# Sums of FFN weight blocks: from VectorE instructions to accumulating DMAs issued by GpSimd

## The chip, the cores and the metric

The kernel runs on one core of a Trainium2 chip. The metric is the device time of one execution in microseconds. A core has TensorE (PE, matmuls; PEld is its weight load), VectorE (DVE), ScalarE (ACT), GpSimd (POOL) and SyncE (SP), which here issues all DMAs; 16 DMA engines carry them. Each engine works through its own queue in order, and waits at the head of it for the semaphores of others.

## The reference, cut to what matters

A two-layer encoder step (a Mamba-2 SSD layer, then an HGRN2 layer), each mixer followed by a SwiGLU FFN, for 1024 prompt tokens and 32 sample tokens, D_MODEL 1024, FFN_HIDDEN 2816, all in float32. The change is in the FFN:

```python
def swiglu(h, w_gate, w_up, w_down):
    return (jax.nn.silu(h @ w_gate) * (h @ w_up)) @ w_down
...
            x = x + out.astype(x.dtype)
            x = x + swiglu(rmsnorm(x, ffn_norm_w[layer]), ffn_w_gate[layer], ffn_w_up[layer], ffn_w_down[layer])
```

## The kernel before, in words

The 1056 tokens go in two halves of 512 and 544 columns; a half is split in two again, n = 256 or 272. Every float32 operand is split into a high and a low part (`wh`/`wl`, `xh`/`xl`), and a product is three matmuls: high by high, high by low, low by high.

The FFN's hidden columns come in 11 slabs of 256. In each half the first one or two slabs go the plain way (`ffn_head`). The others are computed as units, one for the gate and one for the up product: `ffn_unit` multiplies a weight block of 1024 x 256 by a half in Strassen's manner (Winograd's form). The weight slab is cut into four blocks a11, a12, a21, a22 of 512 x 128 (rows 0 to 511 or 512 to 1023, columns 0 to 127 or 128 to 255), the activations into four likewise, and seven products take the place of eight. Each of the seven is a `part`: 4 row blocks by 3 matmuls, 12 matmuls (lines 1003 to 1005). The activation side of the sums is made once for each half by `x_combos` (tiles `th`, `tl`); the weight side for each unit by `unit_weights`. There are 18 units in a first half and 20 in a second one, 76 in both layers, with 2128 x 3 matmuls.

`unit_raw` (line 959) loads the slab by two DMAs of 512 KB (rows of 1 KB) into two `raw` tiles, or into the one Y tile, in turn: gate units in `raw` (three slots), upper units in Y (one). `unit_weights` (line 973) then makes, with four VectorE instructions over 128 x 512, the sums s1 = a21 + a22, s3 = a11 - a21, s2 = s1 - a11 and s4 = a12 - s2, in place where it can, and hands out in the order a11, s1, a12, s2, s4, s3, a22 the split pairs: `hl` is one copy by ScalarE (`wh`, 128 x 512) and one subtraction by VectorE, into one of six `ws` slots. As all helpers call one function for each operation, line 101 of the profile stands for any VectorE `tensor_tensor`, line 98 for any ScalarE activation, line 104 for `scalar_tensor_tensor` and line 110 for any DMA.

`in_turn` interleaves the generators of two neighbouring units: parts 4 and 5 of one, part 1 of the next, part 6, parts 2 and 3, part 7. After each two slabs (four units, 28 parts) the down product of a pair of slabs, `ffn_outs`, comes in; it runs behind part 7 of the first gate unit of the pair that follows, with part 3 of the upper unit beside it already done. It needs four down weights of 512 KB (`wload`, a `raw` slot and two `ws` slots each) and has 96 matmuls of 512 columns in the first half, 192 of 272 in the second (lines 316 to 318).

The order on each engine is made by a planner from the order of the program, priorities and its own estimate of durations; a tile's slot is given on when its last reader is done. SP's queue holds all DMAs in that planned order. POOL issues none; its few instructions belong to the start and to the SSD layer.

Of the kernel before, what the change touches and what calls it, by code (L numbers as in the profile page):

```python
# [8 lines left out]
F32 = mybir.dt.float32  # L9
F32R = mybir.dt.float32r  # L10
U32 = mybir.dt.uint32
AF = mybir.ActivationFunctionType
# [4 lines left out]
P = 128  # L17
# [24 lines left out]
TW = 552  # L42
# [6 lines left out]
def trunk_kernel(ctx, tc, x_prompt, x_sample, state_ssd, cache_conv, state_hgrn,  # L49
# [5 lines left out]
    V, A, G, PE = nc.vector, nc.scalar, nc.gpsimd, nc.tensor  # L55
# [3 lines left out]
    wp = ctx.enter_context(tc.tile_pool(name="wp", bufs=1))  # L59
# [6 lines left out]
    def nm(s):  # L66
        uid[0] += 1
        return f"{s}_{uid[0]}"

    def T(tag, s, dt=F32):  # L70
        return tp.tile([P, WIDTH[tag]], dt, tag=tag, bufs=BUFS[tag], name=nm(s))
# [25 lines left out]
    def act(out, in_, f, **kw):  # L97
        A.activation(out=out, in_=in_, func=f, **kw)  # L98

    def tt(out, a, b, op, eng=None):  # L100
        (eng or V).tensor_tensor(out=out, in0=a, in1=b, op=op)  # L101

    def stt(out, a, s, b, op0, op1):
        V.scalar_tensor_tensor(out=out, in0=a, scalar=s, in1=b, op0=op0, op1=op1)  # L104
# [4 lines left out]
    def dma(out, in_):  # L109
        nc.sync.dma_start(out=out, in_=in_)  # L110
# [14 lines left out]
    MUL, ADD, SUB = ALU.mult, ALU.add, ALU.subtract  # L125
# [5 lines left out]
    def place(w):  # L131
        used[0] += -(-w // 16) * 16
        return fixed[:, used[0] - -(-w // 16) * 16:][:, :w]
# [23 lines left out]
    for i in range(2):  # L157
        t = place(P)
# [125 lines left out]
    def split(xf, w, pair):  # L284
        xh, xl = pair
        act(xh[:, :w], xf, AF.Copy)
        tt(xl[:, :w], xf, xh[:, :w].bitcast(F32), SUB)
        return pair
# [102 lines left out]
    st = [place(TW) for _ in range(NG)]  # L391
# [540 lines left out]
    def x_combos(h, xn, tx, kept=None):  # L932


        L, n = LEN[h], LEN[h] // 2

        def piece(k):
            xf = []
            for m in (k, k + 4):
                if kept:  # L940
                    xf.append(kept[m])
                    continue
                f = T("n", "xf")
                tt(f[:, :L], xn[m][0].bitcast(F32)[:, :L], xn[m][1].bitcast(F32)[:, :L], ADD)
                xf.append(f)
            b11, b12, b21, b22 = [f[:, q * n:(q + 1) * n] for f in xf for q in range(2)]
            t, u = T("w", "xt"), T("w", "xt")
            tt(t[:, :n], b12, b11, SUB)
            tt(t[:, n:L], b22, t[:, :n], SUB)
            tt(u[:, :n], b22, b12, SUB)  # L950
            tt(u[:, n:L], b21, t[:, n:L], SUB)
            for q, f in enumerate((t, u)):
                tags = [XN2[4 * k + 2 * q], XN2[4 * k + 2 * q + 1]]
                tx[2 * k + q] = split(f[:, :L], L, (T(tags[0], "th", F32R), T(tags[1], "tl", F32R)))
        return [lambda k=k: piece(k) for k in range(4)]

    NU = [0]

    def unit_raw(src):

        if NU[0] % 2:
            t = sp.tile([P, 4 * TW], F32, tag="Y", bufs=1, name=nm("raw2"))
            halves = [t[:, q * 1024:(q + 1) * 1024] for q in range(2)]
        else:
            halves = [wp.tile([P, 2 * TW], F32, tag="raw", bufs=3, name=nm("raw"))[:, :1024] for _ in range(2)]
        out = []
        for q in range(2):
            r3 = halves[q].rearrange("p (k c) -> p k c", k=4)
            dma(r3, src[q * 512:(q + 1) * 512, :].rearrange("(k p) c -> p k c", p=P))
            out.append([r3[:, :, i * P:(i + 1) * P] for i in range(2)])  # L970
        return out

    def unit_weights(src):

        (a11, a21), (a12, a22) = unit_raw(src)

        def hl(x):
            w = wp.tile([P, 2 * TW], F32R, tag="ws", bufs=6, name=nm("wh"))[:, :1024]
            v = w.rearrange("p (q k c) -> p q k c", q=2, k=4)
            act(v[:, 0], x, AF.Copy)  # L980
            tt(v[:, 1], x, v[:, 0].bitcast(F32), SUB)
            return v[:, 0], v[:, 1]

        NU[0] += 1
        s1 = st[NU[0] % 2][:, :512].rearrange("p (k c) -> p k c", k=4)
        yield hl(a11)
        tt(s1, a21, a22, ADD)
        yield hl(s1)
        yield hl(a12)
        tt(a21, a11, a21, SUB)  # L990
        tt(a11, s1, a11, SUB)
        yield hl(a11)
        tt(s1, a12, a11, SUB)
        yield hl(s1)
        yield hl(a21)
        yield hl(a22)

    def part(ps, n, w, xs, more):

# [7 lines left out]
    def ffn_unit(h, src, xn, tx, tag, after):  # L1007


        n = LEN[h] // 2  # L1010
        w = unit_weights(src)
        lo, hi = slice(0, n), slice(n, 2 * n)
        t12, t34 = tx[0::2], tx[1::2]
        px = psum_mm((0, 1))
        s12, s35 = T("n", "s12"), T("n", "s35")

        def of(tiles, q):
            return [(a[:, q * n:(q + 1) * n], b[:, q * n:(q + 1) * n]) for a, b in tiles]

        part(px, n, next(w), of(xn[:4], 0), False)  # L1020
        act(s12[:, lo], px[:, :n], AF.Copy)
        yield
        py, pz = psum_sc(), psum_sc()
        part(py, n, next(w), of(t12, 0), False)
        act(s35[:, hi], py[:, :n], AF.Copy)
        part(pz, n, next(w), of(xn[4:], 0), False)
        yield
        dst = [T(tag, "f" + tag) for _ in range(2)]
        tt(dst[0][:, lo], pz[:, :n], s12[:, lo], ADD)
        part(px, n, next(w), of(t12, 1), True)  # L1030
        act(s12[:, hi], px[:, :n], AF.Copy)
        part(py, n, next(w), of(xn[4:], 1), True)
        tt(dst[0][:, hi], py[:, :n], s12[:, hi], ADD)
        yield
        part(px, n, next(w), of(t34, 0), True)
        act(s35[:, lo], px[:, :n], AF.Copy)
        tt(dst[1][:, hi], s35[:, lo], s35[:, hi], ADD)
        yield
        part(px, n, next(w), of(t34, 1), True)
        act(dst[1][:, lo], px[:, :n], AF.Copy)  # L1040
        after(dst)
# [19 lines left out]
    def ffn_gate(layer, h, s, xn, tx, g):  # L1061
        L = LEN[h]

        def after(dst):
            g.extend(dst)
            for x in g:
                act(x[:, :L], x[:, :L], AF.Silu)
        return ffn_unit(h, ffn_w_gate[layer][:, s * 256:(s + 1) * 256], xn, tx, "w", after)

    def ffn_upper(layer, h, s, xn, tx, g, hid):  # L1070
        L = LEN[h]

        def after(dst):
            for x, y in zip(g, dst):
                tt(y[:, :L], x[:, :L], y[:, :L], MUL)
                hid.append(split(y[:, :L], L, (T("ys", "fh", F32R), T("ys", "fl", F32R))))
        return ffn_unit(h, ffn_w_up[layer][:, s * 256:(s + 1) * 256], xn, tx, "xd", after)

# [273 lines left out]
```

## Time and profile before

| | |
|---|---|
| median of 3 runs | 2867.38 us (2866.68 to 2868.51) |
| span of the profiled execution | 2867.3 us, one execution on core 0 |
| TensorE busy | 2838.4 us, 99%, 19704 matmuls |
| VectorE busy | 2131.5 us, 74% |
| ScalarE busy | 1560.3 us, 54% |
| GpSimd busy | 44.1 us, 2% |
| DMA | 281.56 MB, 394518 packets, mean 98 GB/s; the one queue of SP 33.6% of 16 engines |
| granted TensorE clock | 0.999 (mean) |

The span is that of one profiled execution, and it is as long as the median run. A row of the groups has line, engine, operation, out<-in by the program's names with shapes, xcount | busy us, mean ns of one | idle time of the engine before them and what ended it. In rows of waits stand the engine and what it would do, what it waited for, us in total, times and the longest one. Rows of windows give for a stretch its length and each engine's busy time with the number of instructions, then the granted clock, the busy share of the DMA engines and GB/s. Rows of the timeline give start us, us, engine, line, operation. Rows of DMA issues end with KB of one and the median us from issue to landing. Matmuls overlap, so the duration of one is longer than the distance to the next.

### The profile page before, as it was taken

To read this page: it belongs to the slowest core of one execution; us is meant where nothing else is said; L and a number is where in the kernel's file an instruction comes from. 1 tells how busy PE (TensorE), PEld (TensorE's weight loads), DVE (VectorE), ACT (ScalarE), POOL (GpSimd) and SP (SyncE) were. 2 spreads that over 40 slices of the span, in tenths; PEclk is the share of its full clock that TensorE was granted. 3 is DMA by queue.
4 is the path that set the end of the run, shared out by engine and by line. 5 is a ranking of instruction groups with operands and counts; after the bars stand their busy time and mean duration, and the time that the engine had idled before them with its cause. 6 is when DMAs were issued, how large, how long until landed. Compare 5 with 4: busy or idle time off the path is not lost.

```text
span 2867.3 us, 48953 instructions
## 1 busy us (share of the span) xinstructions
PE 2838.4 (99%) x19704; PEld 2614.7 (91%) x19704; DVE 2131.5 (74%) x3686; ACT 1560.3 (54%) x2910; POOL 44.1 (2%) x156
## 2 busy tenths in 40 slices
PE   8999999999999999999999999999999999999998
PEld 8778788999979999999999887899988999999998
DVE  7787887787787877797777556655568877787776
ACT  6665654564644644465444656555564644455544
POOL 1000000000100000000000000000000000000000
PEclk9999999999999999999999999999999999999999
DMA  6444334444322332333323222222222432333332
GB/s 185 111 114 110 95 103 109 115 112 106 103 79 89 119 103 89 111 93 99 96 89 108 81 74 66 75 79 74 80 79 83 124 97 89 117 93 111 104 96 69
DMA packets 394518, 281.56 MB, mean 98 GB/s; under 512 B 16289, under 2 KB 382514, under 8 KB 394290
## 3 DMA queue, kind: packets, MB, share of 16 engines
q1 hardware_dynamic: 394290, 278.43, 33.6%
q8 instruction: 154, 2.52, 0.4%
q14 instruction: 74, 0.61, 0.1%
HBM read 270.57 MB, written 7.82 MB: 97 GB/s over the span
## 4 chain that ended last, share of the span: by engine, by line
PE 93%; DVE 4%; ACT 2%; issue 1%; DMA 0%; SPq 0%; POOL 0%; DVEq 0%; ACTq 0%
PE mm L316 19%; PE mm L317 19%; PE mm L318 19%; PE mm L1005 5%; PE mm L1003 5%; PE mm L1004 5%; PE sc L1005 4%; PE sc L1004 4%; PE sc L1003 4%; PE sc L582 1%; PE sc L571 1%; PE sc L333 1%; PE sc L568 1%; DVE ca L104 1%; PE mm L1277 1%
## 5 line engine op out<-in xcount | busy, mean ns | idle before, releaser
L98 ACT ACTIVATE wh<-raw 128x512 fp32r<-128x512 f32 (+1 forms) x687 | 554.8, 816 | 592.8 <-PE mm L317 491.3
L316 PE MATMUL mm<-xn,wh 128*128 128x272 f32 (+2 forms) x1552 | 523.4, 338 | 1.2 <-ACT pre L98 1.2
L318 PE MATMUL mm<-xn,wl 128*128 128x272 f32 (+2 forms) x1552 | 517.1, 333 | 1.4 <-DVE wl L101 1.4
L317 PE MATMUL mm<-xn,wh 128*128 128x272 f32 (+2 forms) x1552 | 517.9, 334 | 0.0
L101 DVE TENSOR_TENSOR wl<-raw,wh 128x1024 fp32r<-128x1024 f32 (+1 forms) x307 | 372.8, 1216 | 73.8 <-ACT wh L98 52.1
L101 DVE TENSOR_TENSOR fixed<-mm,fixed 128x272 f32<-128x272 f32 (+3 forms) x504 | 259.0, 524 | 199.5 <-PE mm L318 193.3
L316 PE MATMUL mm<-fh,wh 128*128 128x272 f32 (+1 forms) x992 | 322.6, 327 | 0.4 <-ACT fh L98 0.3
L317 PE MATMUL mm<-fl,wh 128*128 128x272 f32 (+1 forms) x992 | 322.7, 326 | 0.0
L318 PE MATMUL mm<-fh,wl 128*128 128x272 f32 (+1 forms) x992 | 322.4, 326 | 0.0
L316 PEld LDWEIGHTS mm<-xn,wh 128*128 128x128 f32 x1552 | 291.8, 188 | 30.9 <-issue 3.0
L318 PEld LDWEIGHTS mm<-xn,wl 128*128 128x128 f32 x1552 | 291.8, 188 | 30.3 <-DVE wl L101 1.8
L317 PEld LDWEIGHTS mm<-xn,wh 128*128 128x128 f32 x1552 | 292.1, 188 | 27.0 <-issue 1.0
L101 DVE TENSOR_TENSOR wh<-raw,wh 128x512 fp32r<-128x512 f32 x380 | 255.8, 685 | 36.6 <-ACT wh L98 33.2
L1003 PE MATMUL mm<-th,wh 128*128 128x272 f32 (+1 forms) x912 | 260.7, 286 | 0.0
L1005 PE MATMUL mm<-th,wh 128*128 128x272 f32 (+1 forms) x912 | 259.9, 285 | 0.0
L1004 PE MATMUL mm<-tl,wh 128*128 128x272 f32 (+1 forms) x912 | 259.6, 285 | 0.0
L316 PEld LDWEIGHTS mm<-fh,wh 128*128 128x128 f32 x992 | 186.3, 188 | 17.1 <-ACT fh L98 1.9
L318 PEld LDWEIGHTS mm<-fh,wl 128*128 128x128 f32 x992 | 186.5, 188 | 15.2
L317 PEld LDWEIGHTS mm<-fl,wh 128*128 128x128 f32 x992 | 186.6, 188 | 14.9 <-DVE fl L101 0.2
L1003 PE MATMUL sc<-xn,wh 128*128 128x272 f32 (+1 forms) x608 | 172.9, 284 | 0.5 <-ACT wh L98 0.5
L1003 PEld LDWEIGHTS mm<-th,wh 128*128 128x128 f32 x912 | 171.8, 188 | 1.6 <-ACT s L98 1.1
L1004 PE MATMUL sc<-xn,wh 128*128 128x272 f32 (+1 forms) x608 | 173.3, 285 | 0.0
(266 smaller groups left out, 6696.6 us busy)
## 6 DMA issues: line engine op xcount, KB each, us to landing
raw<-in_ffn_w_gate_dram SPq DMA_DIRECT2D x88, 512.0 KB, 4.0
raw<-in_ffn_w_up_dram SPq DMA_DIRECT2D x88, 512.0 KB, 4.7
raw<-in_ffn_w_down_dram SPq DMA_DIRECT2D x88, 512.0 KB, 3.5
raw<-in_ssd_in_w_dram SPq DMA_DIRECT2D x80, 512.0 KB, 4.1
raw<-in_hgrn_in_w_dram SPq DMA_DIRECT2D x64, 512.0 KB, 4.2
cumB<-cumd SPq DMA_DIRECT2D x64, 256.0 KB, 4.9
raw<-in_ssd_out_w_dram SPq DMA_DIRECT2D x32, 512.0 KB, 3.7
raw<-in_hgrn_out_w_dram SPq DMA_DIRECT2D x16, 512.0 KB, 3.3
```

What stands on the lines that cost most here:

```text
L98: A.activation(out=out, in_=in_, func=f, **kw)
L101: (eng or V).tensor_tensor(out=out, in0=a, in1=b, op=op)
L104: V.scalar_tensor_tensor(out=out, in0=a, scalar=s, in1=b, op0=op0, op1=op1)
L316: PE.matmul(ps[:, :bn], a, mh, start=(k == 0), stop=False)
L317: PE.matmul(ps[:, :bn], a, ml, start=False, stop=False)
L318: PE.matmul(ps[:, :bn], b, mh, start=False, stop=(k == n - 1))
L333: PE.matmul(ps[:, :bn], ones, tot[:, b0:b0 + bn], start=True, stop=True)
L568: PE.matmul(y23[:, j, :n], S[:, j * P:(j + 1) * P], Cx, start=True, stop=True)
L571: PE.matmul(pp, Btok[:n, :], xw[:n, :], start=True, stop=True)
L1003: PE.matmul(ps[:, :n], a, mh, start=(k == 0 and not more), stop=False, skip_group_check=True)
L1004: PE.matmul(ps[:, :n], a, ml, start=False, stop=False, skip_group_check=True)
L1005: PE.matmul(ps[:, :n], b, mh, start=False, stop=(k == 3), skip_group_check=True)
```

## The change

`unit_weights` no longer calls VectorE. Each of the seven operands gets a room of 256 KB (128 x 512) of its own: the Y tile has four of them, a piece of `st` one, and a `raw` tile two; a gate unit (odd) takes Y, `st` and one `raw`, an upper unit `st` and three `raw`. SP loads a block into each (a11 three times, a12 twice, a21 and a22 once), and GpSimd issues four DMAs that add to what lies in the room (`accum_op=ADD`): s1 = a21 + a22 and s3 = a11 + a21 with the second term from HBM, s2 = a11 + s1 and s4 = a12 + s2 with the second term from the rooms in SBUF. s3, s2 and s4 now have signs by which all are sums; to make up for them the activation sums t are negated (two `tensor_tensor` of each `x_combos` piece become `scalar_tensor_tensor`), Silu takes the second gate result with scale -1, and the product of the second result takes -1 in a `scalar_tensor_tensor`.

```diff
@@ x_combos
-            tt(t[:, :n], b12, b11, SUB)
-            tt(t[:, n:L], b22, t[:, :n], SUB)
+            tt(t[:, :n], b11, b12, SUB)
+            stt(t[:, n:L], t[:, :n], -1.0, b22, MUL, SUB)
             tt(u[:, :n], b22, b12, SUB)
-            tt(u[:, n:L], b21, t[:, n:L], SUB)
+            stt(u[:, n:L], t[:, n:L], -1.0, b21, MUL, SUB)
...
-    def unit_raw(src):
...
-        for q in range(2):
-            r3 = halves[q].rearrange("p (k c) -> p k c", k=4)
-            dma(r3, src[q * 512:(q + 1) * 512, :].rearrange("(k p) c -> p k c", p=P))
...
     def unit_weights(src):
+        def block(i, q):
+            return src[q * 512:(q + 1) * 512, i * P:(i + 1) * P].rearrange("(k p) c -> p k c", p=P)
+
+        NU[0] += 1
         if NU[0] % 2:
             t = sp.tile([P, 4 * TW], F32, tag="Y", bufs=1, name=nm("raw2"))
+            free = [t[:, q * 512:(q + 1) * 512] for q in range(4)]
         else:
+            free = []
+        free.append(st[NU[0] % 2][:, :512])
+
+        def load(i, q):
+            if not free:
+                t = wp.tile([P, 2 * TW], F32, tag="raw", bufs=3, name=nm("raw"))
+                free.extend(t[:, q * 512:(q + 1) * 512] for q in range(2))
+            t = free.pop(0).rearrange("p (k c) -> p k c", k=4)
+            dma(t, block(i, q))
+            return t
+
+        def plus(t, x):
+            G.dma_start(out=t, in_=x, accum_op=ADD)
+            return t
...
-        s1 = st[NU[0] % 2][:, :512].rearrange("p (k c) -> p k c", k=4)
-        yield hl(a11)
-        tt(s1, a21, a22, ADD)
-        yield hl(s1)
-        yield hl(a12)
-        tt(a21, a11, a21, SUB)
-        tt(a11, s1, a11, SUB)
-        yield hl(a11)
-        tt(s1, a12, a11, SUB)
-        yield hl(s1)
-        yield hl(a21)
-        yield hl(a22)
+        a11 = load(0, 0)
+        s1 = plus(load(1, 0), block(1, 1))
+        a12 = load(0, 1)
+        s2 = plus(load(0, 0), s1)
+        s4 = plus(load(0, 1), s2)
+        s3 = plus(load(0, 0), block(1, 0))
+        a22 = load(1, 1)
+        for x in (a11, s1, a12, s2, s4, s3, a22):
+            yield hl(x)
...
@@ ffn_gate
-            for x in g:
-                act(x[:, :L], x[:, :L], AF.Silu)
+            for x, sign in zip(g, (1.0, -1.0)):
+                act(x[:, :L], x[:, :L], AF.Silu, scale=sign)
@@ ffn_upper
-            for x, y in zip(g, dst):
-                tt(y[:, :L], x[:, :L], y[:, :L], MUL)
+            for i, (x, y) in enumerate(zip(g, dst)):
+                if i:
+                    stt(y[:, :L], y[:, :L], -1.0, x[:, :L], MUL, MUL)
+                else:
+                    tt(y[:, :L], x[:, :L], y[:, :L], MUL)
```

More of the change, by code (lines that the diff above doesn't have):

```diff
@@ L957, in trunk_kernel, with unit_weights @@
     NU = [0]
-    def unit_raw(src):
+    def unit_weights(src):
+        def block(i, q):
+            return src[q * 512:(q + 1) * 512, i * P:(i + 1) * P].rearrange("(k p) c -> p k c", p=P)
+        NU[0] += 1
         if NU[0] % 2:
             t = sp.tile([P, 4 * TW], F32, tag="Y", bufs=1, name=nm("raw2"))
-            halves = [t[:, q * 1024:(q + 1) * 1024] for q in range(2)]
+            free = [t[:, q * 512:(q + 1) * 512] for q in range(4)]
         else:
-            halves = [wp.tile([P, 2 * TW], F32, tag="raw", bufs=3, name=nm("raw"))[:, :1024] for _ in range(2)]
-        out = []
-        for q in range(2):
-            r3 = halves[q].rearrange("p (k c) -> p k c", k=4)
-            dma(r3, src[q * 512:(q + 1) * 512, :].rearrange("(k p) c -> p k c", p=P))
[L970 to L975, printed above, removed]
+            free = []
[10 more added lines that the diff above has]
+            return t
         def hl(x):
@@ L982, in hl @@
             return v[:, 0], v[:, 1]
-        NU[0] += 1
-        s1 = st[NU[0] % 2][:, :512].rearrange("p (k c) -> p k c", k=4)
-        yield hl(a11)
-        tt(s1, a21, a22, ADD)
-        yield hl(s1)
-        yield hl(a12)
-        tt(a21, a11, a21, SUB)
-        tt(a11, s1, a11, SUB)
-        yield hl(a11)
-        tt(s1, a12, a11, SUB)
-        yield hl(s1)
-        yield hl(a21)
-        yield hl(a22)
+        a11 = load(0, 0)
[7 more added lines that the diff above has]
+            yield hl(x)
     def part(ps, n, w, xs, more):
```

## The prediction

> **What bounds the kernel now.** I read the page's busy shares first, then the windows of the four stretches in which the units run, then who waits on TensorE there.
>
> ```profile
> span 2867.3 us, 48953 instructions
> PE 2838.4 (99%) x19704; PEld 2614.7 (91%) x19704; DVE 2131.5 (74%) x3686; ACT 1560.3 (54%) x2910; POOL 44.1 (2%) x156
> ...
> core 0: us, PE busy (x) PEld busy (x) DVE busy (x) ACT busy (x) POOL busy (x), PEclk, DMA share, GB/s
> 900.00:1215.00 315.00, 313.73 (x2171) 290.99 (x2170) 251.34 (x415) 165.13 (x310) 0.00 (x0) 1.00 0.33 101
> 1240.00:1540.00 300.00, 299.98 (x2387) 299.12 (x2386) 232.43 (x398) 162.09 (x301) 0.00 (x0) 1.00 0.32 97
> 2185.00:2500.00 315.00, 315.00 (x2185) 293.04 (x2184) 252.06 (x414) 163.55 (x306) 0.00 (x0) 1.00 0.34 106
> 2530.00:2831.00 301.00, 301.00 (x2407) 300.81 (x2406) 228.44 (x397) 164.11 (x311) 0.00 (x0) 1.00 0.33 103
> sum 1231.00, PE 1229.71 PEld 1183.96 DVE 964.27 ACT 654.89 POOL 0.00; mean PE 307.43 PEld 295.99 DVE 241.07 ACT 163.72 POOL 0.00
> ```
>
> TensorE is busy 1229.71 of the 1231.00 us of these four windows, at full granted clock: 1.3 us idle. VectorE is busy 964 of 1231 us (78%), so the work that the change takes from it stands beside TensorE's, not ahead of it. POOL is empty here, the DMA engines are a third used. The chain of waits says the same: 93% of it is TensorE. The reader sees that nothing in these stretches can be sped up by relieving VectorE; the question is only whether the new way of making the sums can be kept as well hidden as the old one.
>
> How it is hidden now: ScalarE's splits run ahead of TensorE, and wait for a free `ws` slot, not for data.
>
> ```profile
> ACT wh L98 <- PE mm L317: 563.3, 166, 5.1
> ...
> DVE fixed L101 <- DMA raw<-in_ffn_w_gate_dram: 32.6, 22, 3.2
> ACT wh L98 <- DMA raw<-in_ffn_w_up_dram: 28.6, 32, 1.7
> ```
>
> 563 us of waiting for TensorE against some 61 us for the units' DMAs, none of which reaches TensorE. The lead is at most six parts (`ws` has six slots, one for each part of a unit).
>
> **The rhythm.** Units come four at a time, then one stage of `ffn_outs`. In the timeline of TensorE the first matmul of each side:
>
> ```profile
> 1000.36 0.39 PE L316 MATMUL mm<-fh,wh 128*128 128x512 f32 x1
> 1022.61 0.28 PE L1003 MATMUL mm<-th,wh 128*128 128x256 f32 x1
> 1062.30 0.39 PE L316 MATMUL mm<-fh,wh 128*128 128x512 f32 x1
> ...
> 1313.30 0.69 PE L1003 MATMUL mm<-th,wh 128*128 128x272 f32 x1
> 1355.96 0.29 PE L316 MATMUL mm<-fh,wh 128*128 128x272 f32 x1
> 1380.15 0.29 PE L1003 MATMUL mm<-th,wh 128*128 128x272 f32 x1
> ```
>
> In the first half (512 columns) the outs take 22.25 us and the 28 parts of four units 39.69 us, 1.418 us a part; in the second (544 columns) 24.19 and 42.66 us, 1.524 us a part. A period is 61.9 or 66.9 us. With 18 and 20 units to a stretch I count 4 and 5 such periods, 8 and 10 over both layers.
>
> **The change, part by part.** (1) Removed: four sums a unit on VectorE, 76 units.
>
> ```profile
> L101 DVE TENSOR_TENSOR fixed<-raw,raw 128x512 f32<-128x512 f32 x76 | 52.3, 688 | 33.4 <-DMA raw<-in_ffn_w_gate_dram 32.6
> L101 DVE TENSOR_TENSOR fixed<-raw 128x512 f32<-128x512 f32 x76 | 52.2, 686 | 4.5 <-DMA raw<-in_ffn_w_up_dram 4.4
> L101 DVE TENSOR_TENSOR raw<-raw 128x512 f32<-128x512 f32 x76 | 52.1, 685 | 0.8
> L101 DVE TENSOR_TENSOR raw<-fixed,raw 128x512 f32<-128x512 f32 x76 | 51.9, 683 | 0.3
> ...
> L104 DVE SCALAR_TENSOR_TENSOR ca<-pre,fixed,ca 128x547 f32<-128x547 f32 x72 | 56.5, 785 | 7.5 <-ACT ca L98 6.4
> L101 DVE TENSOR_TENSOR fxd<-fw,fxd 128x544 f32<-128x544 f32 x40 | 28.8, 720 | 0.5
> ```
>
> That is 208.5 us of VectorE work, worth nothing on the path beyond a part of the 1.3 us above: 0.
>
> (2) The turned signs. Where `tensor_tensor` becomes `scalar_tensor_tensor`, the last two rows give 65 ns more for a full width: 38 products of the upper units, 2.5 us, inside what (1) frees; 32 half-width ones in `x_combos`, at most 2.1 us in all, beside TensorE's head pieces: 0. The `scale` of Silu adds no instruction. If (1)'s room were gone, these would cost 4.6 us of VectorE.
>
> (3) Loads. Seven of 256 KB a unit instead of two of 512 KB. Every issue takes SP's time, and each block of 128 columns lands in half-length rows.
>
> ```profile
> raw<-in_ffn_w_gate_dram SPq DMA_DIRECT2D x88, 512.0 KB, 4.0
> raw<-in_ffn_w_up_dram SPq DMA_DIRECT2D x88, 512.0 KB, 4.7
> raw<-in_ffn_w_down_dram SPq DMA_DIRECT2D x88, 512.0 KB, 3.5
> cumB<-cumd SPq DMA_DIRECT2D x64, 256.0 KB, 4.9
> fixed<-in_x_prompt_dram SPq DMA_DIRECT2D x16, 256.0 KB, 5.2
> out_dram<-yo SPq DMA_DIRECT2D x16, 256.0 KB, 2.0
> ...
> 1319.57 0.92 SPq L110 DMA_DIRECT2D raw<-in_ffn_w_up_dram  x2
> ...
> 1354.47 11.08 SPq L110 DMA_DIRECT2D raw<-in_ffn_w_gate_dram  x3
> ```
>
> SP takes 0.46 us an issue: 3.2 us a unit instead of 0.9, of a unit's 9.9 to 10.7 us of TensorE; hidden by SP's idle time, and the down loads queue 2.3 us longer behind them. HBM reads grow from 1.05 to 2.36 MB a unit (nine blocks). In 900 to 1215 the 0.33 share moved 101 GB/s, 31.8 MB; 18 units add 23.6 MB, and the two sums of SBUF blocks 9.4 MB: share about 0.67, and 0.87 if an accumulating DMA also reads its destination through the engines. Not yet the bound, but landings will not get quicker.
>
> (4) Room. A gate unit now holds the Y tile and one `raw`, an upper unit all three `raw` (before: two `raw`, and Y). The outs' down weights find no `raw` kept free: the first can be loaded only when part 3 of the upper unit is split. I take 0, since the splits' lead covers it; without that cover it costs a landing and a split, 3.5 us + ScalarE's and VectorE's passes, about 6 us for each of 18 outs.
>
> (5) Four accumulating DMAs a unit on POOL's queue, in this order: s1 (needs the load of a21), s2 (needs s1), s4 (needs s2), s3 (needs a load into the last `raw`). Each waits at the head of POOL's queue, and all behind it wait too, the next unit's s1 included. Call A the time from its issue to its landing, I the part in which POOL is held. A unit then keeps the queue for A (s1) + A (s2) + I (s4) + I (s3) = 2A + 2I, and its s4 lands 3A after its start.
>
> No row of this trace has a DMA issued by POOL. Bounds: not under 2.0 us (a 256 KB store); a sum that costs nothing on VectorE can't bring a gain here, as (1) shows. From above, two passes of the slowest 256 KB load, 2 x 5.2 = 10.4 us. Between them the unit's own load is nearest: 512 rows and 512 KB read, as much as an accumulation reads from its source and its destination; of the two medians I take the later, 4.7 us, for the fuller queues of (3). For I the row is POOL's own longest instruction:
>
> ```profile
> L101 POOL TENSOR_TENSOR fixed<-fixed 128x4 f32<-128x4 f32 x1 | 1.0, 1008 | 1.1 <-DVE fixed L107 1.1
> L98 ACT ACTIVATE wh<-raw 128x512 fp32r<-128x512 f32 x382 | 235.0, 625 | 192.1 <-PE mm L317 140.6 <-DMA raw<-in_ffn_w_up_dram 28.6 <-PE sc L1005 6.6
> ```
>
> I = 1.0, A = 1.0 + 4.7 = 5.7. (SP's 0.46 would be the low end of I, twice the row the high one.)
>
> The sum, in us after the start of an outs stage. The next gate unit's loads go out until 1354.47 + 11.08 = 1365.55, 9.6 us after the outs began at 1355.96; with 4.0 to land, its s1 starts at 14. The unit number j (0, 1, 2) after the outs starts at 14 + 13.4 j, and its s4 lands at 14 + 13.4 j + 17.1: 31.1, 44.5, 57.9. TensorE needs s4 at part 5, which for these units are the parts 8, 15 and 22 after the outs; a split before it takes 0.63 (ScalarE, above) + 0.69 (VectorE). Due: outs + 1.418 (8 + 7 j) - 1.3 = 32.3, 42.2, 52.1 in the first half; 35.1, 45.7, 56.4 in the second. First half: the second unit is 2.3 late, the third then 57.9 - 54.4 = 3.5: 5.8 us a period. Second half: only the third, 1.5 us. The other sums fall due later than they land (s1 of the third unit: 46.5 against 48.8), and the fourth unit's s4 comes behind the next outs, which is why the loss doesn't grow. 8 x 5.8 + 10 x 1.5 = 61 us. With 2867.3 before: 2929 us. The profiled span agrees with the runs' median of 2867.38, so nothing is added for that.
>
> What the sum hangs on is A: at A = 4.0, I = 1.0 a unit takes 10 us and s4 lands at 26, 36, 46, all in time: 0. At A = 5.0: 29, 41, 53: about 1 us in the first half alone, 8 us. At A = 7, I = 1.5 the unit takes 17 us, s4 lands at 35, 52, 69: 16.9 and 12.6 us a period, 261 us. At A = 10.4, I = 1 four units take 91.2 us, 29.3 and 24.3 more than a period: about 480 us.
>
> The landings above are all SP's. The Trainium skill, "DMA: Bandwidth & Descriptors", section on the anatomy of one DMA on the GpSimd path, gives 2.0 us plus bytes / 436e3 for a DMA that GpSimd issues: as an estimate 2.6 us for 256 KB, and by it the sum is 0. [...]
>
> **The rivals.** *Hidden anyway.* Place: POOL's queue. For it: POOL is empty in the four windows, a store of 256 KB lands in 2.0 us, the planner may put the next unit's Y loads ahead of the down loads and so start s1 before 14, and VectorE, 10 us freer in a burst, lets the splits lead again sooner. Against: three landings in a row where VectorE took 0.7 us each. It decides at A below about 4.8: 2867 us. The page cited above would put the change here.
>
> *Queue-bound.* Place: the same queue. If A is over some 7.4, or the DMA engines are full by the upper share of (3), four units no longer fit into a period at all, and TensorE waits in every unit: 3180 to 3350 us.
>
> *Faster.* One mechanism: the planner, with the sums off VectorE, lets evacuations and norms come earlier where TensorE waits for VectorE and ScalarE. But the units' windows hold only 1.3 us of idle time; outside them idle time is 2867.3 - 2838.4 - 1.3 = 27.6 us, in the start, the mixers and the tail, which the change does not touch. It decides only if over 5.7 us of that goes: 2860 us.
>
> **How the numbers follow.** 0.2% is 5.7 us, about what a measurement of this kernel can tell from no change. Stalls in the bursts (the forecast, own range 2875 to 3130, A from 5 to 7): 0.48. Hidden anyway: 0.30. Queue-bound: 0.17. Faster: 0.04. Other slips that cost time, such as (4): 0.01. So faster 0.04, same 0.30, slower 0.66. The range runs from 2864, just under the hidden case, to 3180, A about 7.4, and leaves out most of the queue-bound case and half of the faster one.
>
> **What would show it.** VectorE's busy time down by some 200 us; POOL's queue waiting for DMAs, with a chain POOL, DMA, POOL ahead of ScalarE's `wh`; idle time of TensorE in front of L1003 in the bursts, none in the outs; the DMA share of the windows near two thirds. The time to compare with A is the landing of POOL's issues. If these land under 4 us, or TensorE's windows stay full, the forecast is wrong; likewise if the idle time stands before L316, where the down weights come late.

## The result, and the profile after

The changed kernel takes 3160.73 us in the median (3157.94 to 3170.37) against 2867.03 for the kernel before in the same comparison: ratio 1.1029, interval 1.1016 to 1.1043. That is 294 us slower; the forecast was 62 us slower. The profiled execution took 3161.45 us.

The page of the kernel after, its first lines, and two of its windows (columns as in the windows of the prediction):

```profile
span 3159.6 us, 50458 instructions
...
PE 2929.1 (93%) x19704; PEld 2686.5 (85%) x19704; DVE 1961.1 (62%) x3382; ACT 1556.5 (49%) x2910; POOL 374.3 (12%) x460
...
900.00:1280.00 380.00, 331.56 (x2129) 303.31 (x2128) 209.64 (x337) 163.52 (x308) 76.41 (x71) 0.92 0.75 167
...
1900.00:2300.00 400.00, 395.25 (x2760) 366.55 (x2760) 247.43 (x514) 236.80 (x405) 0.00 (x0) 1.00 0.27 77
```

Two things grew. TensorE's idle time (span less busy) went from 28.9 to 3159.6 - 2929.1 = 230.5 us: 201.6 more. And the same 19704 matmuls were busy 90.7 us longer, 2929.1 against 2838.4, since the granted clock fell, to 0.92 in the window full of units. In 1900 to 2300, which holds no GpSimd work, it is 1.00, with 4.75 us of idle time. 201.6 + 90.7 = 292 us: this is the whole difference between the two spans.

Who waited in the kernel after:

```profile
ACT wh L98 <- PE mm L317: 469.2, 166, 7.4
...
ACT wh L98 <- DMA raw<-in_ffn_w_down_dram: 281.3, 58, 10.6
...
ACT wh L98 <- DMA raw<-in_ffn_w_up_dram: 165.9, 23, 11.5
...
SPq L110 <- DMA raw<-raw: 204.0, 52, 6.8
...
PE mm L316 <- DVE fxd L101: 65.3, 16, 9.8
PE mm L1006 <- DVE fxd L101: 41.1, 7, 7.9
PE mm L1006 <- ACT s L98: 39.2, 19, 5.0
PE mm L1006 <- ACT fw L98: 36.2, 7, 7.7
PE sc L1006 <- ACT s L98: 14.4, 6, 5.4
```

The unit's matmul lines 1003 to 1005 are now 1006 to 1008. TensorE's new waits are 65.3 us before the down products (L316) and 41.1 + 39.2 + 36.2 + 14.4 = 130.9 us in the bursts of units (L1006). None of the five is ended by a split (`wh`, `wl`). All are ended by evacuations (`s`, `fw`, `fxd`), the instructions that read a finished sum out of PSUM. In the kernel before no such wait sums to more than 6 us. ScalarE in turn waits for DMAs at its splits: 281.3 us for the down weights, where the kernel before has 6.6 us in four waits, and 165.9 us for blocks of the upper units. SP waits 204.0 us for transfers from room to room.

The chain of waits of the kernel after, in the 18 us up to one of the stalls before the outs (start us, us, what):

```profile
1442.87 6.56 DMA raw<-raw
...
1451.35 6.16 DMA raw<-in_ffn_w_down_dram
...
1459.85 0.36 DVE fxd L101
```

This is the mechanism before the outs, from top to bottom. An accumulating DMA reads a room of a `raw` tile for 6.56 us; only when it has landed is the slot free, and only then can SP issue the loads behind it and the down load (1451.35). That lands 6.16 us later. ScalarE has stood at its split for 6.72 us, and the evacuations are behind the split:

```profile
1457.53 1.06 ACT L98 ACTIVATE wh<-raw 128x1024 fp32r<-128x1024 f32 x1 [6.72 <-DMA raw<-in_ffn_w_down_dram]
1458.50 0.38 ACT L98 ACTIVATE s<-sc 128x272 f32<-128x272 f32 x1
...
1460.35 0.57 PE L316 MATMUL mm<-fh,wh 128*128 128x272 f32 x1 [5.45 <-DVE fxd L101]
1460.71 0.43 PE L317 MATMUL mm<-fl,wh 128*128 128x272 f32 x1
1460.94 0.43 PE L318 MATMUL mm<-fh,wl 128*128 128x272 f32 x1
...
1463.88 0.29 PE L316 MATMUL mm<-fh,wh 128*128 128x272 f32 x1
1464.00 0.29 PE L317 MATMUL mm<-fl,wh 128*128 128x272 f32 x1
```

These are rows of ScalarE's and TensorE's timelines. ScalarE waits 6.72 us for the down weights, then reads `s` out of PSUM; TensorE, which needed that, has waited 5.45 us. After the stall matmuls of 272 columns start every 0.23 us, until 1463.88, and then every 0.12 to 0.13: for 3.5 us TensorE runs at half rate. Such stretches are where the 90.7 us come from. The Trainium skill, "TensorE: Matmul & The Clock Gate", Part 1 (The HAM clock gate), describes it: an activity window of 3.4 us, and half the clock after an idle one until a busy one has passed. The trace agrees, with 3.5 us of half rate behind an idle 5.45. But an idle time of 3.4 us isn't needed here: behind a stall of 1.87 us (up to 1224.32) matmuls of 256 columns start every 0.21 us from 1225.08 to 1228.28, and every 0.12 us after that.

Issues and landings of GpSimd's DMAs in the kernel after; the two L981 rows give the issue's own duration, ns, least/median/most:

```profile
raw<-raw POOLq DMA_DIRECT2D x114, 256.0 KB, 5.6
raw<-in_ffn_w_gate_dram POOLq DMA_DIRECT2D x76, 256.0 KB, 6.0
raw<-in_ffn_w_up_dram POOLq DMA_DIRECT2D x76, 256.0 KB, 5.7
fixed<-raw POOLq DMA_DIRECT2D x38, 256.0 KB, 3.9
...
L981 POOL DMA_DIRECT2D raw<-raw x114: 837/881/1027, 870.0 to 3100.4; - x114
L981 POOL DMA_DIRECT2D raw<-in_ffn_w_gate_dram x76: 1264/1282/2167, 861.4 to 3085.5; - x76
...
DMA to landing us min/median/max: 3.2/5.5/8.4
```

So the prices that the forecast had doubted most were about right: 5.5 us for A (taken 5.7), and in the median 0.85 to 1.61 us for I (taken 1.0; the 1.61 are the issues for the upper units' blocks from HBM). The gap has to come from the schedule in which they stand. In one period, whose outs start at 1460.35, SP's queue has the four down loads ahead of the loads of the units that follow, and each waits for a `raw` slot:

```profile
1451.35 22.05 SPq L110 DMA_DIRECT2D raw<-in_ffn_w_down_dram  x4
1479.14 1.16 SPq L110 DMA_DIRECT2D raw<-in_ffn_w_gate_dram  x2
```

GpSimd's queue around the same outs, and a stall in the units behind them, on ScalarE and TensorE:

```profile
1445.68 1.28 POOL L981 DMA_DIRECT2D raw<-in_ffn_w_gate_dram  x1 [1.93 <-DVE wh L101]
...
1483.12 1.28 POOL L981 DMA_DIRECT2D raw<-in_ffn_w_gate_dram  x1 [21.95 <-DVE fixed L101]
1484.76 1.26 POOL L981 DMA_DIRECT2D raw<-in_ffn_w_up_dram  x1 [0.35 <-DMA raw<-in_ffn_w_up_dram]
...
1509.81 0.85 POOL L981 DMA_DIRECT2D fixed<-raw  x1 [6.54 <-DMA raw<-raw]
1510.35 1.61 POOL L981 DMA_DIRECT2D raw<-in_ffn_w_up_dram  x1
...
1515.44 1.15 ACT L98 ACTIVATE wh<-raw 128x512 fp32r<-128x512 f32 x2 [8.05 <-DMA raw<-in_ffn_w_up_dram]
...
1516.93 0.59 PE L1006 MATMUL mm<-xn,wh 128*128 128x272 f32 x1 [5.51 <-ACT fw L98]
```

Of a unit's DMAs from HBM the first on this queue is s1, the second s3. The next gate unit's s1 leaves at 1445.68, 14.7 us before the outs start, since its loads into Y (from 1440.98) stand ahead of the down loads; the forecast had it 14 us after. What comes 23 us after the start is that unit's s3, whose `raw` slot was taken, and right behind it s1 of the next upper unit: 24 to 26 us in most periods. And the planner has put another unit's chain into this one's: between s1 and s3 of the upper unit stand s1, s2 and s4 of the gate unit after it. So s3 leaves at 1510.35, with its own data there, behind an s4 (`fixed<-raw`) that waited 6.54 us; it lands 55 us after the outs began, ScalarE's split waits 8.05 us for it, and `fw` behind the split holds TensorE for 5.51. This is the main loss in the units: followed back through the trace, 101 of the 131 us at L1006, in 22 waits, end at s3 of an upper unit, and 30 us at s2 or s4 of any unit.

### The profile page after: what moved, and what is told of

Same layout as the page of the kernel before. It is cut to its first block, busy times and chain, and to the rows that moved or that the text cites. A ratio compares the mean times of both kernels' runs of the same rounds, so it can differ in the third digit from the quotient of the medians.

```text
span 3159.6 us, 50458 instructions
## 1 busy us (share of the span) xinstructions
PE 2929.1 (93%) x19704; PEld 2686.5 (85%) x19704; DVE 1961.1 (62%) x3382; ACT 1556.5 (49%) x2910; POOL 374.3 (12%) x460
## 4 chain that ended last, share of the span: by engine, by line
PE 62%; DMA 14%; issue 8%; DVE 8%; ACT 5%; POOL 2%; SPq 1%; POOLq 0%; ACTq 0%; DVEq 0%
PE mm L316 16%; PE mm L318 16%; PE mm L317 16%; DMA raw<-in_ffn_w_down_dram 5%; DMA raw<-in_ffn_w_up_dram 5%; ACT wh L98 2%; DMA raw<-in_ffn_w_gate_dram 2%; DMA raw<-raw 2%; POOL raw L981 2%; DVE wl L101 1%; DVE wh L101 1%; PE mm L1006 1%; PE sc L582 1%; PE mm L1008 1%; PE mm L1007 1%
## 5 line engine op out<-in xcount | busy, mean ns | idle before, releaser
L98 ACT ACTIVATE wh<-raw 128x512 fp32r<-128x512 f32 (+1 forms) x763 | 597.0, 797 | 1069.5 <-PE mm L317 460.9
L316 PE MATMUL mm<-xn,wh 128*128 128x272 f32 (+2 forms) x1552 | 524.2, 338 | 1.8 <-ACT pre L98 1.5
L101 DVE TENSOR_TENSOR wh<-raw,wh 128x512 fp32r<-128x512 f32 x456 | 307.5, 688 | 319.2 <-ACT wh L98 314.4
L316 PE MATMUL mm<-fh,wh 128*128 128x272 f32 (+1 forms) x992 | 335.4, 340 | 66.3 <-DVE fxd L101 65.3
L318 PE MATMUL mm<-fh,wl 128*128 128x272 f32 (+1 forms) x992 | 332.8, 336 | 2.4 <-DVE wl L101 2.3
L317 PE MATMUL mm<-fl,wh 128*128 128x272 f32 (+1 forms) x992 | 333.0, 336 | 0.2 <-DVE fl L101 0.2
L316 PEld LDWEIGHTS mm<-xn,wh 128*128 128x128 f32 x1552 | 291.4, 188 | 31.4 <-issue 2.9
L1006 PE MATMUL mm<-th,wh 128*128 128x272 f32 (+1 forms) x912 | 275.9, 302 | 39.2 <-ACT s L98 39.2
L1007 PE MATMUL mm<-tl,wh 128*128 128x272 f32 (+1 forms) x912 | 271.7, 298 | 0.0
L1008 PE MATMUL mm<-th,wh 128*128 128x272 f32 (+1 forms) x912 | 270.8, 297 | 0.0
L316 PEld LDWEIGHTS mm<-fh,wh 128*128 128x128 f32 x992 | 195.0, 197 | 87.5 <-ACT fw L98 60.7
L981 POOL DMA_DIRECT2D raw<-in_ffn_w_gate_dram x76 | 110.1, 1449 | 1297.1 <-DMA raw<-in_ffn_w_gate_dram 786.2
L1006 PEld LDWEIGHTS mm<-th,wh 128*128 128x128 f32 x912 | 185.1, 203 | 44.8 <-ACT s L98 44.1
L1006 PE MATMUL sc<-xn,wh 128*128 128x272 f32 (+1 forms) x608 | 176.1, 290 | 14.9 <-ACT s L98 14.4
```

Of the source, the lines that this page charges most:

```text
L316: PE.matmul(ps[:, :bn], a, mh, start=(k == 0), stop=False)
L317: PE.matmul(ps[:, :bn], a, ml, start=False, stop=False)
L318: PE.matmul(ps[:, :bn], b, mh, start=False, stop=(k == n - 1))
L981: G.dma_start(out=t, in_=x, accum_op=ADD)
L1006: PE.matmul(ps[:, :n], a, mh, start=(k == 0 and not more), stop=False, skip_group_check=True)
L1007: PE.matmul(ps[:, :n], a, ml, start=False, stop=False, skip_group_check=True)
```

## The experiments

Theory at the start: (a) the down weights come late because the upper unit holds all three `raw` slots (step 4, which the forecast had priced at 0), and SP's queue, standing at them, starts the next unit late; (b) each accumulation is long. Rival: the chain of three accumulations alone, counted from a correct start, is the loss. All ratios are to the kernel before, run beside. In the expectations x1 is run 3 and x3 is run 4.

**1. Only the signs.** The kernel before, with the turned signs and VectorE's four sums.

```diff
-        tt(a21, a11, a21, SUB)
-        tt(a11, s1, a11, SUB)
+        tt(a21, a11, a21, ADD)
+        tt(a11, s1, a11, ADD)
...
-        tt(s1, a12, a11, SUB)
+        tt(s1, a12, a11, ADD)
```

> The kernel before with the turned signs alone: sums of blocks as additions on VectorE, scalar_tensor_tensor in the activation sums and in the product, Silu with scale -1. Every theory: within 5 us of before.

2866.58 us, ratio 0.9998 (0.9989 to 1.0008). The signs cost nothing.

**2. No sums at all.** The kernel after without its four GpSimd transfers; the sums are left out, and raw blocks stand in their place.

```diff
-            G.dma_start(out=t, in_=x, accum_op=ADD)
```

> As x1, but the four sums are left out altogether: the split reads the loaded blocks. Room theory: over 2970 us. Chain theory: 2860 to 2880 us. If x1 is slow and this one fast, it is VectorE's work in the new order, and neither.

2886.89 us, ratio 1.0072 (1.0055 to 1.0089). This is far from the room theory and 7 us above the chain theory's range. Seven loads in seven rooms with three slots cost 20 us by themselves, though ScalarE stands 197.2 us before the down weights; the other 274 us need the accumulations.

**3. The sums on VectorE, in the rooms.** Seven loads stay, VectorE adds. In s1 it adds a12, which is at hand, in place of a22; for s3, a21 is loaded and a11 added.

```diff
-        s2 = plus(load(0, 0), s1)
-        s4 = plus(load(0, 1), s2)
...
+        tt(s2, s2, s1, ADD)
+        yield hl(s2)
+        tt(s4, s4, s2, ADD)
+        yield hl(s4)
```

> The changed kernel's seven loads, rooms and turned signs, but the sums made by four VectorE additions in the rooms, with no DMA from GpSimd (s1 adds a12 in place of a22, so that no room is needed earlier; the work is the same). Room theory (the loss comes from seven loads on SP's queue and from upper units that hold all three raw slots, so that the down weights and the next unit's loads come late): still over 2970 us, with idle time of TensorE before L316 as now. Chain theory (the loss comes from three landings of about 5.5 us in a row where VectorE took 0.7 us each): 2860 to 2885 us.

2927.52 us, ratio 1.0208 (1.0193 to 1.0223). It lies between the two expectations, and both miss: the loads and rooms cost 60 us even with VectorE's quick sums, less than the theory of the rooms wanted, and more than that of the chain allowed. Run 2 has the same loads and rooms and costs 20 us, so some 40 of the 60 come with VectorE's sums in the new rooms (they wait 82.1 us for blocks of the upper units alone), and not with the loads.

**4. A fourth `raw` slot.** `raw` and `ws` tiles cut from 2 x TW to the 1024 columns that are used, which makes room for it; the program is otherwise that of the kernel after.

```diff
-        raw = wp.tile([P, 2 * TW], F32, tag="raw", bufs=3, name=nm("raw"))[:, :1024]
+        raw = wp.tile([P, 1024], F32, tag="raw", bufs=4, name=nm("raw"))[:, :1024]
```

> The changed kernel with four raw slots in place of three; to make room, raw and ws tiles are 1024 columns wide instead of 1104, of which 1024 were used. All accumulating DMAs stay. Room theory: the first s1 after the outs starts near 14 us after their beginning instead of 23, the wait before L316 is gone, 2920 to 2990 us. Chain theory: 3080 to 3165 us.

3056.11 us, ratio 1.0666 (1.0650 to 1.0681): 105 us back. The first accumulations after the outs now leave at 7 to 9 us (s3 of the gate unit) and 12 to 15 us (s1 of the upper unit, as the room theory had it); the wait before L316 is not gone. But the slot is not all that changed: the planner laid out GpSimd's queue anew, with s3 of an upper unit ahead of the next gate unit's s1 (1459.06 and 1461.30 in one period), so that each unit's sums stand together, as the forecast had them. ScalarE's wait for blocks of the upper units falls from 165.9 to 25.5 us. Slot and order aren't told apart by this run. Even so 189 us are lost. Its waits:

```profile
ACT wh L98 <- DMA raw<-in_ffn_w_down_dram: 139.6, 46, 6.3
...
PE mm L1006 <- ACT s L98: 89.3, 36, 4.9
```

And one stall on the timelines of ScalarE and TensorE:

```profile
1496.02 1.06 ACT L98 ACTIVATE wh<-raw 128x1024 fp32r<-128x1024 f32 x1 [5.50 <-DMA raw<-in_ffn_w_down_dram]
1496.98 0.38 ACT L98 ACTIVATE s<-mm 128x272 f32<-128x272 f32 x1
...
1497.41 0.60 PE L1006 MATMUL mm<-th,wh 128*128 128x272 f32 x1 [4.43 <-ACT s L98]
```

Here a unit's part waits 4.43 us for `s`, and `s` stands on ScalarE behind the split of a down weight that TensorE won't need before the outs, some parts later. So a datum was due not when TensorE needed it, but when the in-order queue that touches it first came to it.

**5. A quarter of each sum.** The kernel after, each accumulation cut to its first row block, 64 KB; three quarters of each sum are left out.

```diff
-            G.dma_start(out=t, in_=x, accum_op=ADD)
+            G.dma_start(out=t[:, :1], in_=x[:, :1], accum_op=ADD)
```

> The changed kernel with the same four accumulating DMAs a unit, but each adds only the first of its four row blocks (64 KB in place of 256 KB); three quarters of each sum are left out. Waits, rooms, loads and the order of the queues stay. Chain theory: the landings fall from 5.5 to about 3 to 4 us and with them at least half of the loss: under 3010 us. Room theory: 3090 us or more.

3007.67 us, ratio 1.0489 (1.0474 to 1.0505): 153 us back, with landings of 3.5 us in the median instead of 5.5. The order on GpSimd's queue keeps s3 of an upper unit behind the next gate unit's s4, and the first s1 still starts 23 to 26 us after the outs in most periods. So the length of a landing and the late start can be moved apart.

**6. Both together.** Four slots and quarter sums (three quarters of each sum left out).

> Four raw slots (3056 us alone) and each accumulate cut to its first row block of 64 KB (3008 us alone) together; the other three quarters of each sum are left out. If the two causes, the late start of a unit's transfers and their length, are separate, the savings against 3160 (104 and 153 us) add: 2900 to 2920, and the rest over 2867 is that of the seven loads alone, as in the run with VectorE's sums and four slots (2914). If the two are one cause counted twice (a late landing, however it comes), or if something else in the four GpSimd transfers costs, 2940 to 3000.

2906.51 us, ratio 1.0136 (1.0121 to 1.0151): 254 us back. The two savings alone, 104.6 + 153.1, make 257.7. They add within the intervals, as the theory of two separate causes had it. What is left is 39.5 us; that it is the seven loads alone, as the expectation says, isn't shown, for these cost 20 us in run 2. TensorE's waits and the clock in this run:

```profile
core 0: 2905.1 us, clock 0.998
...
PE mm L316 <- DVE fxd L101: 21.1, 14, 2.8
...
PE mm L1006 <- ACT s L98: 8.4, 9, 2.0
```

No wait of TensorE in the stretches of units is over 2.8 us, and the clock is 0.998: the half-rate stretches went with the long stalls.

**7. Plain copies.** The kernel after, its GpSimd DMAs copying the same bytes and not adding; the sums are not formed.

```diff
-            G.dma_start(out=t, in_=x, accum_op=ADD)
+            G.dma_start(out=t, in_=x)
```

> The kernel after, with its four GpSimd transfers of a unit as plain copies of the same 256 KB from the same sources into the same places, so that the sums are not formed; queues, waits and the order of all instructions stay as they are. Theory A (it is the accumulation, the destination read and written back, that makes a landing of 5.5 to 6 us): landings near the 3.5 us that the quarter-size accumulates showed, and a time near that run's 3008 us, 2990 to 3030. Theory B (the landing is that of 256 KB in 512 rows on GpSimd's queue beside the other loads, whatever is done on arrival): landings 5 to 6 us, time 3130 to 3170.

3054.06 us, ratio 1.0646 (1.0630 to 1.0662). Neither expectation held whole; the first, that accumulation makes the landing long, is the nearer.

```profile
raw<-raw POOLq DMA_DIRECT2D x114, 256.0 KB, 4.7
raw<-in_ffn_w_gate_dram POOLq DMA_DIRECT2D x76, 256.0 KB, 4.2
raw<-in_ffn_w_up_dram POOLq DMA_DIRECT2D x76, 256.0 KB, 3.6
fixed<-raw POOLq DMA_DIRECT2D x38, 256.0 KB, 2.3
...
L981 POOL DMA_DIRECT2D raw<-raw x114: 537/549/559, 870.4 to 2994.7; - x114
L981 POOL DMA_DIRECT2D raw<-in_ffn_w_gate_dram x76: 747/754/940, 862.6 to 2980.3; - x76
```

Of the same 256 KB, accumulating takes 0.9 to 2.1 us longer to land, and holds GpSimd 0.88 and 1.28 us where a copy holds it 0.55 and 0.75. With the same order on GpSimd's queue this is worth 3160.7 - 3054.1 = 107 us over 304 accumulations, 0.35 us each. The DMA engines are less busy too (share 0.47 of the span against 0.56); whether their load lengthens the other landings isn't shown.

**8. A slot of their own for the down weights.** Three `raw` for the units, one more tile for the four down loads.

```diff
-                ws[c] = wload([(0, cols, ffn_w_down[layer][s * 256:s * 256 + nk * P, c * cols:(c + 1) * cols])],
-                              nk, cols)
+                r3 = wp.tile([P, 1024], F32, tag="rawd", bufs=1, name=nm("rawd"))
...
```

> The changed kernel, all accumulating DMAs kept, with three raw slots for the units and one slot of its own for the down weights (four in all, as in x3, raw and ws tiles 1024 columns wide). Coupled theory (a raw slot comes free only when the accumulating DMA that reads it has landed; the down weights then load late, and their split, at the head of ScalarE's queue, holds up the evacuations that TensorE needs): ScalarE's wait for down weights falls under 100 us, 2930 to 3000 us. Chain theory (only the three landings in a row count): as x3, 3040 to 3070 us.

3123.58 us, ratio 1.0888 (1.0869 to 1.0908): a miss for both. The down loads now wait for each other in the one slot, and ScalarE waits 283.2 us for them (281.3 in the kernel after). TensorE's wait before L316 falls from 65.3 to 25.2 us, but SP still has the down loads ahead of the next upper unit's loads, which leave 23 us after the outs began (20 in the kernel after). GpSimd's queue has the order of the kernel after, and ScalarE's wait for blocks of the upper units stays, 173.0 us. So a slot without the other order gave 37 us, and both together 105.

**9. VectorE's sums with four slots.** Run 3 with run 4's tiles (s1 again with a12 in place of a22).

> x1 (seven loads and rooms, sums by VectorE, s1 adding a12 in place of a22) with four raw slots. If x1's 60 us come from the missing slot: 2867 to 2885 us. If they come from the seven loads (SP's time, the DMA engines' load): 2905 to 2930 us.

2913.64 us, ratio 1.0164 (1.0149 to 1.0179). The fourth slot takes ScalarE's wait for the down weights from 224.9 to 48.9 us, but only 14 us from the time. So the missing slot is a small part of run 3's 60 us. The time lies in the range of the seven loads, but they cost 20 us in run 2, and the remaining 47 are not all theirs. The rest is left to VectorE's sums; four slots without any sums were not run.

**10. Half and half.** Four slots; s1 and s3 by accumulating DMA, s2 and s4 by VectorE, so that no chain of DMAs is longer than one.

```diff
-        s2 = plus(load(0, 0), s1)
-        s4 = plus(load(0, 1), s2)
+        s2 = load(0, 0)
+        s4 = load(0, 1)
...
+        tt(s2, s2, s1, ADD)
+        yield hl(s2)
+        tt(s4, s4, s2, ADD)
+        yield hl(s4)
```

> s1 and s3 by accumulating DMAs from HBM, s2 and s4 by VectorE in their rooms, four raw slots. One landing in a row instead of three, and no DMA reads a room. Chain and coupled theory: 2880 to 2930 us. If instead the DMA engines' load or GpSimd's number of DMAs is what costs, about half of x3's loss: 2950 to 2970 us.

3180.74 us, ratio 1.1091 (1.1074 to 1.1107): slower than with all four sums by DMA (3056), and the worst miss of all. A chain of one DMA is no gain when VectorE has to wait for it; what the chain's length costs where GpSimd waits for it, this run can't show. Its waits:

```profile
DVE raw L101 <- DMA raw<-in_ffn_w_gate_dram: 266.7, 36, 8.9
...
PE mm L1013 <- ACT s L98: 199.7, 43, 8.2
```

One stall on the timelines of VectorE, ScalarE and TensorE:

```profile
1462.33 0.69 DVE L101 TENSOR_TENSOR raw<-raw 128x512 f32<-128x512 f32 x1 [8.40 <-DMA raw<-in_ffn_w_gate_dram]
1462.94 0.72 DVE L104 SCALAR_TENSOR_TENSOR fxd<-fxd,fw 128x544 f32<-128x544 f32 x1
...
1463.69 0.66 ACT L98 ACTIVATE fh<-fxd 128x544 fp32r<-128x544 f32 x1 [9.97 <-DVE fxd L104]
...
1464.69 0.60 PE L1013 MATMUL mm<-th,wh 128*128 128x272 f32 x1 [7.41 <-ACT s L98]
```

Four queues stand behind one DMA: VectorE's sum waits 8.40 us for the accumulation, the gate product `fxd` behind it on VectorE, ScalarE's `fh` waits for that (9.97), `s` behind `fh`, and TensorE for `s` (7.41). With four slots, a DMA that feeds the head of VectorE's queue cost more (3181 us) than one that feeds GpSimd's (3056), which had nothing else to do.

**11. and 12. Four `ws` slots instead of six**, in the kernel after, and as a control in the kernel before.

```diff
-            w = wp.tile([P, 2 * TW], F32R, tag="ws", bufs=6, name=nm("wh"))[:, :1024]
+            w = wp.tile([P, 1024], F32R, tag="ws", bufs=4, name=nm("wh"))[:, :1024]
```

> The kernel after with four slots for split weights instead of six, so that ScalarE and VectorE can have at most four parts' splits ahead of TensorE in their queues. Theory head-of-line (a late sum stops the queue at a split whose part is far ahead, and the evacuations behind it with it): the splits stand nearer to their parts, the sums have up to two parts, 3 us, more time, each stall shrinks by up to that: 3050 to 3130. Theory lead (TensorE waits for its own next weights, and the splits' lead is the cover): less lead, more waiting: 3160 to 3260.

> Control for the run before it: the kernel before with four slots for split weights instead of six. Both theories: here the data are there in time, so 2865 to 2885; what it costs over 2867 is to be taken from the other run's time.

3151.39 us, ratio 1.0991 (1.0969 to 1.1014); the control 2864.06, ratio 0.9988 (0.9978 to 0.9997). Both theories fell. The row of the run with four slots shows why it tells nothing of the lead:

```profile
ACT wh L98 <- PE mm L317: 469.4, 170, 5.7
```

It is the kernel after's row (469.2) again: two slots fewer do not make ScalarE wait longer for TensorE, while in the control the same row grows from 563.3 to 642.6 us. With four `raw` slots (run 4) it is 656.5. This speaks for `raw` and not `ws` as the limit of the lead in the changed kernel. How much of the loss head-of-line waiting makes, apart from lateness itself, stays open: it is shown in the rows of runs 4 and 10 and of the kernel after, but no run took it away alone. Moving evacuations ahead of splits, or s3 ahead of the next unit's s1 with three slots, in the planner's order wasn't tried.

## Why the prediction was right and wrong

Right: the direction, and why. The 208.5 us taken from VectorE brought nothing (VectorE's busy time fell by 170, TensorE waited more). The signs were free (run 1). A and I came nearly as worked out. The DMA share did not: 0.75 looks like the forecast's 0.67 to 0.87, but it is of a window of 380 us and not of 315. That is 285 us of engine time, where the forecast's shares make 211 to 274.

The rival *hidden anyway*, which needed A under 4.8, fell with A at 5.5, though its premise on the planner came true: the next gate unit's Y loads do go ahead of the down loads. The price from the Trainium skill, "DMA: Bandwidth & Descriptors" (anatomy of one DMA on the GpSimd path), as an estimate 2.6 us for 256 KB, is near the plain copies' fastest group, 2.3 (the others 3.6 to 4.7); the accumulating ones in these queues landed in 3.9 to 6.0, and the measurement decides. *Queue-bound* came nearest in size (3180 to 3350) but not in cause: A was not over 7.4, and the DMA engines were at 0.75.

Wrong, in the forecast's own terms, 62 us against 294:

- **Step 4, room taken as 0.** Measured: 65.3 us of TensorE waiting before L316, the place that the forecast itself had named as the sign of its failure; its price "without cover", 18 x 6 = 108 us, was the better bound. The cover, the splits' lead, was gone because the accumulation keeps the `raw` slot until it has landed.
- **Step 5, the order of the queue, and which sum is late.** The forecast let a unit's four sums stand together, took s4 for the one that comes late, and said that the other sums fall due later than they land. Its time for s4 of the second unit was near: 45.3 us after the outs began in the period shown, forecast 44.5. But the next gate unit's s1, s2 and s4 stand ahead of the second unit's s3. By the forecast's own A and I that s3 would land at 27.4 + 2 x 5.7 + 1.0 + 5.7 = 45.5; it landed at 55.1. At this sum end 101 us of TensorE's waits, at s2 and s4 only 30.
- **Step 5, the due times.** "1.3 us before the part" reckoned with TensorE's need. ScalarE and VectorE come to a split or a sum earlier than that, and a wait there holds the evacuations behind it, as in run 4. How much of the 130.9 us at L1006 this adds isn't shown: at 1516.93 TensorE stood only one part ahead of the part that needs the late s3, so most of that stall was lateness by the forecast's own rule.
- **No term for the clock.** 90.7 us of longer TensorE busy time: most stalls of 2 us and more in the units' stretches are followed by some 3 to 6 us at half rate. The forecast took a stall at its length.

65.3 + 130.9 + 90.7 = 287 of the 294 us. Cut by cause rather than by place, the runs give: the missing fourth slot, with the order planned around it, 105; the length of the four accumulating transfers 153 (copies of full size that don't add save 107); some 40 left, of which the seven loads alone make 20 in run 2. What the slot and the order are worth each stays open; run 8, with a fourth slot and the old order, gave 37.

## What to carry to other kernels

Taking work from an engine that isn't the bound was worth nothing here, and a DMA in its place keeps its source slot and its destination busy for the whole landing: count slots before microseconds, for a fourth `raw` slot and the order that came with it were worth 105 us here. Write down the planned order of each in-order queue before adding up times: the sum that stood behind another unit's chain held TensorE for 101 us. A transfer is due when the first queue that touches it reaches it; ask what stands behind that instruction, evacuations above all. And a stall of TensorE of a few us is to be priced with the half rate after it, here 90.7 us on 201.6.

## What was not expected of the hardware

- An accumulating DMA of 256 KB holds GpSimd 0.88 us in the median with its source in SBUF, and 1.28 (gate) or 1.61 (upper units) with its source in HBM; a plain one 0.55 and 0.75. It lands in 5.5 us in the median, least 3.2; a quarter of the size still needs 3.5.
- The busy time of TensorE is not a constant of the work: the same 19704 matmuls took 2838.4 us at a mean granted clock of 0.999, 2845.6 (run 6) at 0.998, and 2929.1 in the kernel after at 0.963.
